# Low parts of the merge gates' weight slabs: an accumulating transfer in place of a subtraction

## The chip, the cores and the metric

The kernel runs on one core of a Trainium2 chip. Its time is the device time of one execution in microseconds (us), taken as the median over several runs. The names used below: PE is the matrix engine (PEld its weight loads), DVE the vector engine, ACT the scalar engine, POOL the GpSimd engine, SP the engine that issues most of the transfers. A line number such as L454 is a line of the kernel before.

## What is computed

One layer of a hybrid encoder: an input projection whose columns feed attention, a gated delta rule run in both directions, and two merge gates; the two branches are gated, summed and projected, and a second gated term is added. Cut to what bears on the change (512 positions, model width 1024, float32):

```python
h = rms_norm(x, norm_pre[i])
(aq, ak, av, az, dq, dk, dv, db, da, dz, gate_att, gate_dn) = split_cols(h @ w_in[i])
...
y_att = (o_att * jax.nn.silu(az)) @ w_br_att[i]
...
y_dn = (o_dn * jax.nn.silu(dz)) @ w_br_dn[i]
mix = (jax.nn.sigmoid(gate_att) * y_att + jax.nn.sigmoid(gate_dn) * y_dn) @ w_out[i]
x = x + rms_norm(mix, norm_post[i])
e = p[i] @ w_ple_proj[i]
x = x + rms_norm(jax.nn.sigmoid(x @ w_ple_gate[i]) * e, ple_norm[i])
```

`gate_att` and `gate_dn` are the two merge gates. Their weights are 2048 columns of `w_in`.

## The kernel before, in words

Every large product is made of three products in a shorter float format (float32r): a weight tile w is split into a high part `hi`, which is w rounded to that format, and a low part `lo` = w - `hi`; the activations are split in the same way, and PE adds lo x high, high x low and high x high into one accumulator.

**Slabs.** The weights come as 72 slabs of 128 columns (1024 x 128, as a tile of 128 x 1024 numbers, 512 KB), named by kind and number: dk, dq, dv, dz, az, gA (merge gate of the attention branch), gB (merge gate of the delta branch), ydn, yatt, with eight of each. Blocks of 512 columns (kv, q0, q1, out0, out1, pg0, pg1) come in four pieces of the same size each. `fetch` issues the loads into the tile `wraw` (two buffers) on SP's queue. `loader` follows: it takes one `whi` and one `wlo` buffer (two of each), calls `split`, which has ACT cast `wraw` to `whi` and then DVE or POOL subtract (`wlo` = `wraw` - `whi`), and gives `wraw` back. `gemm_t` runs a slab's 24 matmuls on PE, eight rounds of L454 (low part), L455 and L456 (high part), and gives `whi` and `wlo` back in the last round. `gemm_k` does so for kv and q0, q1 (L489 to L491), `gemm_n` for the last four blocks (L471 to L473), whose parts lie in buffers of their own (u).

**Order.** `ORDER` is a list written out by hand, by which one generator (`stream`) walks through the slabs and blocks, one after the other. Everything else (the delta rule's two chains, one for each group of four heads; attention; what follows each slab) is made of other generators. A planner in Python (`Flow`) runs them all against a clock of its own at build time: each operation is booked on its engine with an estimated duration, at the first gap that fits; a generator waits for events, for buffers (`get`) or for a time; among those that are ready the one with the lowest priority number goes first, and the stream has 10, the chains 1. The order of those bookings becomes the order of the instructions on each engine, which is then fixed; on the chip an instruction waits for its data by semaphores. A booking on both DVE and POOL (`W`) makes the planner keep both free, though only one of them works.

**Where a low part is made.** `split` with `sbuf=True` works out when the subtraction would end on DVE (1024 x 0.00113 us, with POOL kept free) and on POOL (1024 x 0.00232 us), and takes POOL if that ends sooner than the other way plus `COOL` (1.5 us), or plus `HOT` (0 us) while a chain's triangular solve is under way (`chains[0]`); in the first 20 us of the planner's clock always POOL (`slow`).

**The chains.** Each chain (one after the other) makes decay matrices (`phase_a`: transfers of CI, an addition on DVE, a select and a product on POOL, then matmuls L828 and L833), solves triangular systems with 30 dependent steps on DVE, and then runs `phase_b` (L985 to L1037). `phase_y` norms the chain's result and transposes it (L1095). The tails of q0 and q1 rotate and transpose (L1250), the convolutions' tails transpose (L686). After q1 the eight attention heads run (L1339), then the yatt slabs, out0, out1, pg0 and pg1. A merge gate's result goes through a tanh to the DRAM tensors gate_gA and gate_gB and is read back much later, in `ydn_tail` and `yatt_tail`.

**Norm vectors.** The item `vec` of `ORDER`, which stands after yatt5 and yatt6, starts two `vec_load` generators that load the weights of the last two norms into `blk` buffers (three in all, used by the heads as well). Each yatt job waits for `att_start` and for all eight heads before its matmuls.

Of the kernel before, what the change touches and what calls it, by code (L numbers as in the profile page):

```python
# [9 lines left out]
F32 = mybir.dt.float32  # L10
F32R = mybir.dt.float32r
AF = mybir.ActivationFunctionType
ALU = mybir.AluOpType
# [21 lines left out]
class Flow:  # L35
# [39 lines left out]
    def op(self, eng, dur, dep, fn, *a, **k):  # L75

        engs = eng if isinstance(eng, tuple) else (eng,)
        t, at = self.slot(engs, dur, dep)
        for e, i in zip(engs, at):
            self.eng[e].insert(i, (t, t + dur))  # L80
        if fn is not None:
            self.n += 1
            heapq.heappush(self.later, (t, self.n, fn, a, k))
        return t + dur

    def free(self, tag, t=None):
        self.slots[tag].append(self.now if t is None else t)
# [61 lines left out]
X_DVE = ()  # L149
WARM = 9  # L150
W1 = 0
COOL, HOT = 1.5, 0


@with_exitstack
def layer(ctx, tc, x, p, wt, wba, wn, wpp, npre, rows, qkn, hd16, npost, pnorm, dnorm, cs, out):
    nc = tc.nc
    pe, act, dve, pool, sync = nc.tensor, nc.scalar, nc.vector, nc.gpsimd, nc.sync

    caps = {"wraw": 2, "whi": 2, "wlo": 2, "f2": 5, "c2": 4, "blk": 3, "gi": 2, "go": 2, "mm": 5, "aux": 3}  # L160
    F = Flow({**caps, **{f"u{i}": 1 for i in range(17)}})
    op, free, spawn = F.op, F.free, F.spawn

    def A(dur, dep, fn, *a, **k):
        return op("ACT", dur, dep, fn, *a, **k)
# [8 lines left out]
    def G(dur, dep, fn, *a, **k):  # L174
        return op("POOL", dur, dep, fn, *a, **k)

    def Q(kb, dep, o, i):

        t = op("DGE", 0.46, dep, sync.dma_start, o, i)
        return op("DMA", kb * 0.364, t + 0.5, None) + 1.0  # L180

    sb = ctx.enter_context(tc.tile_pool(name="sb", bufs=1))
    ps = ctx.enter_context(tc.tile_pool(name="ps", bufs=1, space=bass.MemoryType.PSUM))
# [3 lines left out]
    def tile(tag, shape, dt=F32):  # L187
        cnt[0] += 1
        return sb.tile(list(shape), dt, tag=tag, bufs=caps.get(tag, 1), name=f"{tag}_{cnt[0]}")

    def const(shape, name, dt=F32):
        return sb.tile(shape, dt, tag=name, bufs=1, name=name)

    def unit(i, shape, dt=F32):
        return tile(f"u{i}", shape, dt)
# [12 lines left out]

    chains = [0]

    def split(src, hi, lo, dep, n, sbuf=False, slow=False):

        t = A(0.08 + n * 0.00085, dep, act.copy, hi, src)
        eng = "DVE"
        if sbuf:
            eng = ("DVE", "POOL")
            tv = F.slot(eng, n * 0.00113, t)[0] + n * 0.00113
            tp = F.slot(("POOL",), n * 0.00232, t)[0] + n * 0.00232
            if slow or tp < tv + (HOT if chains[0] else COOL):
                eng = "POOL"  # L220
        fn = (pool if eng == "POOL" else dve).tensor_sub
        t2 = op(eng, n * (0.00232 if eng == "POOL" else 0.00113), t, fn, lo, src, hi.bitcast(F32))
        return t, t2

    def bc(a):
        return a.unsqueeze(2).to_broadcast([128, 4, 128])
# [5 lines left out]
    def row(src, n):  # L232
        return src.rearrange("(o n) -> o n", o=1).broadcast_to([128, n])
# [12 lines left out]
    two = const([64, 32], "two")  # L246
# [35 lines left out]
    load, ple, late = {}, {}, {}  # L282
# [8 lines left out]
    def first_loads():  # L291
# [4 lines left out]
        def p_half(i):  # L296
            ple["tp"].append(Q(2, 0.0, ple["p"][:, 2 * i:2 * i + 2], p[256 * i:256 * i + 256].rearrange("(t p) n -> p t n", p=128)))
# [3 lines left out]
        def ple_weights(half):  # L301
            raw = tile("wraw", [128, 2, 512])
            load["ple", half] = raw, Q(4, 0.0, raw, wpp.rearrange("(j p) n -> p j n", p=128)[:, :, half * 512:half * 512 + 512])
            fetched["ple", half].set(F.now)

        def x_tile(t):
            if t % 2 == 0:
                xu.append(unit(4 + t // 2, [128, 2, D]))
            xt = xu[t // 2][:, t % 2, :]
            load["x", t] = xt, Q(4, 0.0, xt, x[t * 128:(t + 1) * 128, :])  # L310
# [24 lines left out]
    def h_part():  # L335
# [29 lines left out]
        for t in range(NT):  # L365
            xt = load["x", t][0]
            for half in range(2):
                yield "at", sc[t, half] + 0.3
                yield "get", "aux"
                pt = bank("aux", [128, 4, 128])  # L370
                for j in range(4):
                    k = half * 4 + j
                    pe.transpose(pt[:, j, :], xt[:, k * 128:(k + 1) * 128], ident)
                yield "pe", 0.45
                cc = slice(t * 128, (t + 1) * 128)
                _, te = split(pt, hTh[half][:, :, cc], hTl[half][:, :, cc], F.now, 512)
                free("aux", te)
                if t == NT - 1:
                    h_ev[half].set(te + 0.2)
# [17 lines left out]
    def fetch(names):  # L397
        for name in names:
            if name[0] == "ple":
                continue  # L400
            yield "get", "wraw"
            if name[0] == "blk":
                raw = tile("wraw", [128, 2, 512])
                j = name[2]
                src = wn[BLOCK_IDX[name[1]]][:, 2 * j:2 * j + 2, :]
            else:
                raw = tile("wraw", [128, 8, 128])
                src = wt[SLAB_IDX[name]]
            load[name] = raw, Q(4, 0.0, raw, src)
            fetched[name].set(F.now)  # L410

    def loader(names):
        for name in names:
            yield "ev", fetched[name]
            raw, t = load[name]
            sh = [128, 8, 128] if name[0] not in ("blk", "ple") else [128, 2, 512]
            if name[:2] in places or name[0] == "ple":
                if name[0] == "ple":
                    us = (7 + name[1], 7 + name[1])
                    yield "get", f"u{us[0]}"  # L420
                    w = unit(us[0], [128, 2, 2, 512], F32R)
                    hi, lo = w[:, 0], w[:, 1]
                else:
                    us, j = places[name[:2]], name[2]
                    his, los = blocks.setdefault(name[1], ([], []))
                    if j % 2 == 0:
                        for u, lst in ((us[j // 2], his), (us[j // 2 + 2], los)):
                            yield "get", f"u{u}"
                            lst.append(unit(u, [128, 4, 512], F32R))
                    a = (j % 2) * 2  # L430
                    hi, lo = his[-1][:, a:a + 2, :], los[-1][:, a:a + 2, :]
            else:
                yield "get", "whi"
                yield "get", "wlo"
                hi = tile("whi", sh, F32R)
                lo = tile("wlo", sh, F32R)
            yield "at", t - 0.3
            _, tl = split(raw, hi, lo, t, 1024, True, F.now < 20.0)
            free("wraw", tl)
            slab[name][0].set(tl + 0.2)  # L440
            slab[name][1] = (hi, lo)

# [121 lines left out]
    def decay():  # L564
# [4 lines left out]
        wb, t = load["wb"]  # L569
        ws = tile("f2", [128, 8, 64], F32R)  # L570
        _, t = split(wb, ws[:, :, 0:32], ws[:, :, 32:64], t, 256, True)
        free("f2", t)
        yield "at", t + 0.2
# [712 lines left out]
    head_ev = {}  # L1286
    att_start = Event()
# [168 lines left out]
        return rs, G(0.8, dep, fn)  # L1456

    def vec_load(name, src, scale=1.0):
        yield "get", "blk"
        v = late[name] = tile("blk", [128, D])  # L1460
        t = Q(4, 0.0, v, row(src, D))
        if scale != 1.0:
            yield "at", t - 0.5
            t = G(1.5, t, pool.tensor_scalar, out=v, in0=v, scalar1=scale, scalar2=0.0, op0=ALU.mult, op1=ALU.add)
        return t
# [144 lines left out]
    def late_vectors():  # L1610
        late["npo_ev"] = spawn(vec_load("npo", npost), 4)
        late["pno_ev"] = spawn(vec_load("pno", pnorm, 0.5), 4)
# [32 lines left out]
    for n in names:  # L1645
        slab[n] = [Event(), None]
        fetched[n] = Event()
    spawn(fetch(names), 2)
    spawn(loader(names), 2)

    def stream():
# [57 lines left out]
```

## Time and profile before

| | us |
|---|---|
| median of 3 runs (lowest, highest) | 807.49 (805.36, 807.97) |
| the profiled execution's own time | 806.62 |
| its span, first to last instruction | 804.9 |
| PE busy | 764.8 |
| DVE busy | 485.5 |
| POOL busy | 354.0 |
| ACT busy | 316.4 |

The mean granted PE clock of the profiled execution is 0.984 of full speed. Transfers move 96.69 MB, and their packets take 37.8% of the 16 transfer engines' span. The span is what the profiler saw between the first and the last instruction; the execution's own time is 1.7 us longer. In rows of the time line the columns are the start in us, the duration in us, engine, line and operation, what is written and what is read, and in brackets the engine's idle time before it and what ended that. Many operations are recorded by one helper, so that their line is L101; the tile's name tells them apart.

### The profile page before, as it was taken

To read this page: it belongs to the slowest core of one execution; us is meant where nothing else is said; L and a number is where in the kernel's file an instruction comes from. 1 tells how busy PE (TensorE), PEld (TensorE's weight loads), DVE (VectorE), ACT (ScalarE), POOL (GpSimd) and SP (SyncE) were. 2 spreads that over 40 slices of the span, in tenths; PEclk is the share of its full clock that TensorE was granted. 3 is DMA by queue.
4 is the path that set the end of the run, shared out by engine and by line. 5 is a ranking of instruction groups with operands and counts; after the bars stand their busy time and mean duration, and the time that the engine had idled before them with its cause. 6 is when DMAs were issued, how large, how long until landed. Compare 5 with 4: busy or idle time off the path is not lost.

```text
span 804.9 us, 11746 instructions
## 1 busy us (share of the span) xinstructions
PE 764.8 (95%) x4522; PEld 634.8 (79%) x4522; DVE 485.5 (60%) x902; ACT 316.4 (39%) x522; POOL 354.0 (44%) x305
## 2 busy tenths in 40 slices
PE   8998999999999996999999989898999999799995
PEld 6787888887888975878787877686888888678884
DVE  4466777978667567596748554638656633723434
ACT  6454514336334143233452233334656533331421
POOL 6344492014125359502522257655566464560431
PEclk9999999999999998999999999999999999899998
DMA  7372226453212271645411232333253347643213
GB/s 258 114 216 92 78 86 164 126 174 95 67 31 75 79 198 64 170 143 165 133 41 52 80 110 80 105 104 105 79 178 110 118 145 245 207 132 122 92 40 130
DMA packets 52969, 96.69 MB, mean 120 GB/s; under 512 B 20849, under 2 KB 22449, under 8 KB 52914
## 3 DMA queue, kind: packets, MB, share of 16 engines
q1 hardware_dynamic: 52914, 95.95, 37.8%
q8 instruction: 35, 0.57, 0.3%
q14 instruction: 20, 0.16, 0.1%
HBM read 79.12 MB, written 16.81 MB: 119 GB/s over the span
## 4 chain that ended last, share of the span: by engine, by line
PE 75%; DVE 9%; DMA 5%; POOL 4%; issue 3%; ACT 3%; SPq 0%; POOLq 0%; DVEq 0%; ACTq 0%
PE mm L454 12%; PE mm L456 12%; PE mm L455 12%; PE mm L471 4%; PE mm L473 4%; PE mm L472 4%; DVE f L101 4%; PE mm L489 2%; PE mm L491 2%; PE mm L490 2%; DVE u L101 2%; POOL u L101 2%; PE mm L1339 2%; PE aux L1005 2%; PE aux L1037 2%
## 5 line engine op out<-in xcount | busy, mean ns | idle before, releaser
L101 POOL TENSOR_TENSOR wlo<-wraw,whi 128x1024 fp32r<-128x1024 f32 x70 | 168.1, 2403 | 294.7 <-ACT whi L101 291.1
L454 PE MATMUL mm<-u,wlo 128*128 128x512 f32 x576 | 233.5, 405 | 5.6 <-POOL wlo L101 5.6
L456 PE MATMUL mm<-u,whi 128*128 128x512 f32 x576 | 225.6, 392 | 0.0
L455 PE MATMUL mm<-u,whi 128*128 128x512 f32 x576 | 225.0, 391 | 0.0
L101 ACT CAST whi<-wraw 128x1024 fp32r<-128x1024 f32 x84 | 88.2, 1050 | 165.2 <-PE mm L456 106.4
L454 PEld LDWEIGHTS mm<-u,wlo 128*128 128x128 f32 x576 | 108.7, 189 | 26.6 <-POOL wlo L101 6.9
L456 PEld LDWEIGHTS mm<-u,whi 128*128 128x128 f32 x576 | 108.4, 188 | 23.7
L455 PEld LDWEIGHTS mm<-u,whi 128*128 128x128 f32 x576 | 108.8, 189 | 19.6
L101 DVE SCALAR_TENSOR_TENSOR f<-mm,cw,f 128x510 f32<-128x510 f32 (+1 forms) x96 | 71.9, 748 | 23.5 <-ACT f L101 21.0
L471 PE MATMUL mm<-u,u 128*128 128x512 f32 x128 | 51.6, 403 | 4.8 <-DVE u L101 4.8
L101 POOL TENSOR_TENSOR u<-wraw,u 128x1024 fp32r<-128x1024 f32 x18 | 44.4, 2474 | 16.3 <-ACT u L101 16.1
L473 PE MATMUL mm<-u,u 128*128 128x512 f32 x128 | 50.6, 396 | 0.0
L472 PE MATMUL mm<-u,u 128*128 128x512 f32 x128 | 50.5, 395 | 0.0
L101 DVE TENSOR_TENSOR u<-aux,u 128x512 f32<-128x512 f32 (+1 forms) x48 | 32.0, 688 | 22.7 <-ACT u L101 12.5
L101 ACT ACTIVATE f<-mm 128x512 f32<-128x512 f32 (+1 forms) x44 | 24.8, 579 | 48.6 <-PE mm L473 39.9
L489 PE MATMUL mm<-whi,u 128*128 128x512 f32 x96 | 39.2, 408 | 0.0
L490 PE MATMUL mm<-wlo,u 128*128 128x512 f32 x96 | 38.0, 396 | 1.2 <-POOL wlo L101 1.2
L491 PE MATMUL mm<-whi,u 128*128 128x512 f32 x96 | 38.1, 396 | 0.0
L471 PEld LDWEIGHTS mm<-u,u 128*128 128x128 f32 x128 | 24.4, 191 | 10.6 <-DVE u L101 5.8
L101 ACT COPY c<-aux 128x512 f32<-128x512 f32 x18 | 10.7, 592 | 49.9 <-DVE f L101 23.2
L101 DVE TENSOR_TENSOR blk<-mm,blk 128x512 fp32r<-128x512 f32 x32 | 21.2, 687 | 12.9 <-ACT blk L101 12.9
L473 PEld LDWEIGHTS mm<-u,u 128*128 128x128 f32 x128 | 24.4, 191 | 5.4
(253 smaller groups left out, 1296.9 us busy)
## 6 DMA issues: line engine op xcount, KB each, us to landing
wraw<-in_wt_dram SPq DMA_DIRECT2D x72, 512.0 KB, 3.4
wraw<-in_wn_dram SPq DMA_DIRECT2D x28, 512.0 KB, 3.9
u<-CI SPq DMA_DIRECT2D x16, 256.0 KB, 6.1
u<-in_x_dram SPq DMA_DIRECT2D x4, 512.0 KB, 7.7
eD<-c SPq DMA_DIRECT2D x8, 256.0 KB, 2.2
gate_az<-go SPq DMA_DIRECT2D x8, 256.0 KB, 3.4
gate_dz<-go SPq DMA_DIRECT2D x8, 256.0 KB, 2.1
gate_gB<-go SPq DMA_DIRECT2D x8, 256.0 KB, 2.0
```

The costliest lines, as they stand in the source:

```text
L101: fn(*a, **k)
L454: pe.matmul(o, lo[:, k, :], mh(k), start=(k == 0), stop=False)
L455: pe.matmul(o, hi[:, k, :], ml(k), start=False, stop=False)
L456: pe.matmul(o, hi[:, k, :], mh(k), start=False, stop=(k == 7))
L471: pe.matmul(o, b, hi, start=(k == 0), stop=False)
L472: pe.matmul(o, a, lo, start=False, stop=False)
L473: pe.matmul(o, a, hi, start=False, stop=(k == 7))
L489: pe.matmul(o[t], b, hi, start=(k == 0), stop=False)
L490: pe.matmul(o[t], a, lo, start=False, stop=False)
L491: pe.matmul(o[t], a, hi, start=False, stop=(k == 7))
L1005: pe.matmul(pw[:, h, :], Vm[g][d][:, 4 * c + h, :], r[:, h, :], start=True, stop=True)
L1037: pe.matmul(oa[:, h, :], AT[g][d][:, 4 * c + h, :], w[:, h, :], start=True, stop=True)
```

## The change

For slabs of the kinds gA and gB, once the planner's clock is past 30 us, a third way of making the low part stands beside the two subtractions. ACT casts `wraw` to `whi` as before, and `wraw` is given back at once. ACT then writes -`whi` into `wlo`, and POOL issues a transfer that reads the slab from DRAM a second time and adds it into `wlo`. `BIAS` is added to the planned end of each way (DVE, POOL, transfer; the first triple outside a triangular solve, the second during one), and the earliest wins; the transfer has -9 us in both. The planner books for it 0.95 us of ACT, 1.1 us of POOL, and 2.9 us of the transfer engines with 0.65 us ahead and 1.5 us behind.

The other slabs choose between DVE and POOL as before; the rule that forces POOL in the first 20 us is gone, and the planned durations are rounded (0.9504 to 0.95, 1.157 to 1.16, 2.376 to 2.38). `vec_load` waits for `att_start` and for the eight heads. `ORDER` is the same.

```diff
-COOL, HOT = 1.5, 0
+BIAS = ((1.5, 0, -9), (0, 0, -9))
+BYDMA = ("gA", "gB")
...
+    def P(kb, dep, o, i):
+
+        t = op("POOL", 1.1, dep, pool.dma_start, o, i, accum_op=ALU.add)
+        return op("DMA", 2 * kb * 0.364, t + 0.5, None) + 1.5
+
...
-    def split(src, hi, lo, dep, n, sbuf=False, slow=False):
+    def split(src, hi, lo, dep, n, sbuf=False):
 
         t = A(0.08 + n * 0.00085, dep, act.copy, hi, src)
-        eng = "DVE"
-        if sbuf:
-            eng = ("DVE", "POOL")
-            tv = F.slot(eng, n * 0.00113, t)[0] + n * 0.00113
-            tp = F.slot(("POOL",), n * 0.00232, t)[0] + n * 0.00232
-            if slow or tp < tv + (HOT if chains[0] else COOL):
-                eng = "POOL"
-        fn = (pool if eng == "POOL" else dve).tensor_sub
-        t2 = op(eng, n * (0.00232 if eng == "POOL" else 0.00113), t, fn, lo, src, hi.bitcast(F32))
-        return t, t2
+        return t, (W if sbuf else V)(n * 0.00113, t, dve.tensor_sub, lo, src, hi.bitcast(F32))
...
-            load[name] = raw, Q(4, 0.0, raw, src)
+            load[name] = raw, Q(4, 0.0, raw, src), src
...
             yield "at", t - 0.3
-            _, tl = split(raw, hi, lo, t, 1024, True, F.now < 20.0)
-            free("wraw", tl)
+            th = A(0.95, t, act.copy, hi, raw)
+
+            two = ("DVE", "POOL")
+            ends = [F.slot(two, 1.16, th)[0] + 1.16 + BIAS[min(chains[0], 1)][0], F.slot(("POOL",), 2.38, th)[0] + 2.38 + BIAS[min(chains[0], 1)][1]]
+            if name[0] in BYDMA and F.now > 30.0:
+                ta = F.slot(("ACT",), 0.95, th)[0] + 0.95
+                tp = F.slot(("POOL",), 1.1, ta)[0] + 1.6
+                ends.append(F.slot(("DMA",), 2.9, tp)[0] + 4.4 + BIAS[min(chains[0], 1)][2])
+            way = ends.index(min(ends))
+            if way == 2:
+                free("wraw", th)
+                tl = A(0.95, th, act.mul, lo, hi.bitcast(F32), -1.0)
+                tl = P(4, tl, lo, load[name][2])
+            else:
+                tl = op((two, "POOL")[way], (1.16, 2.38)[way], th, (dve, pool)[way].tensor_sub, lo, raw, hi.bitcast(F32))
+                free("wraw", tl)
             slab[name][0].set(tl + 0.2)
...
     def vec_load(name, src, scale=1.0):
+        yield "ev", att_start
+        for h in range(8):
+            yield "ev", head_ev[h]
         yield "get", "blk"
```

`split` is also called for tiles of 256 and 512 numbers that are no weights (activations in SBUF with `sbuf=True`). There the choice between DVE and POOL falls away: the subtraction is booked on both and runs on DVE.

More of the change, by code (lines that the diff above doesn't have):

```diff
@@ L414, in loader @@
             yield "ev", fetched[name]
-            raw, t = load[name]
+            raw, t = load[name][:2]
             sh = [128, 8, 128] if name[0] not in ("blk", "ple") else [128, 2, 512]
```

## The prediction

> **What bounds the kernel now.** I read the page first, then PE's waits, then the tile wraw (through which every weight slab passes), and last the time line around single merge-gate slabs.
>
> ```profile
> PE 764.8 (95%) x4522; PEld 634.8 (79%) x4522; DVE 485.5 (60%) x902; ACT 316.4 (39%) x522; POOL 354.0 (44%) x305
> ```
> ```profile
> PE aux L833 <- DVE u L101: 6.5, 2, 5.9
> PE mm L454 <- POOL wlo L101: 5.6, 4, 2.0
> PE mm L471 <- DVE u L101: 4.8, 1, 4.8
> PE mm L1095 <- DVE u L101: 3.5, 4, 1.1
> PE mm L1250 <- DVE f L101: 2.5, 2, 1.4
> ...
> PE mm L490 <- POOL wlo L101: 1.2, 1, 1.2
> PE mm L686 <- DVE f L101: 0.9, 1, 0.9
> ```
>
> PE is busy 764.8 of 804.9 us. The 40 us it lacks are all there is to win, and 4.8 of them lie ahead of out0 (L471), behind the last gate slab. In the list of waits (us in total, times, longest) PE waits for low parts made on POOL for only 5.6 + 1.2 us. POOL and DVE, which the change relieves, are half idle. So the question is whether a gate slab's low part, made the new way, is there when PE wants it.
>
> ```profile
> L101 ACT CAST whi<-wraw x84: 1027/1052/1088, 18.4 to 688.1; 128x1024 fp32r<-128x1024 f32 x84
> ...
> L101 POOL TENSOR_TENSOR wlo<-wraw,whi x70: 2342/2396/2825, 19.6 to 689.2; 128x1024 fp32r<-128x1024 f32 x70
> ...
> L101 DVE TENSOR_TENSOR wlo<-wraw,whi x14: 1217/1223/1226, 133.7 to 371.2; 128x1024 fp32r<-128x1024 f32 x14
> ...
> DMA to landing us min/median/max: 3.0/3.7/8.8
> ```
>
> Today a low part costs 1.05 us on ACT and then 2.40 on POOL or 1.22 on DVE. How long it may take is set by the two whi/wlo buffers: the cast starts when PE has left the slab before last, and PE wants the result when it leaves the last one. Slabs are told apart by counting PE's groups of eight L454 along ORDER. Rows of gB6 (cast, subtraction, first matmul), then cast and first matmul of gA7, gA4, gB3 and gB0, and between them the cast of gB7:
>
> ```profile
> 149.68 0.39 PE L454 MATMUL mm<-u,wlo 128*128 128x512 f32 x1
> 149.88 1.05 ACT L101 CAST whi<-wraw 128x1024 fp32r<-128x1024 f32 x1 [1.69 <-PE mm L456]
> 150.97 1.23 DVE L101 TENSOR_TENSOR wlo<-wraw,whi 128x1024 fp32r<-128x1024 f32 x1 [0.60 <-ACT whi L101]
> 155.12 0.39 PE L454 MATMUL mm<-u,wlo 128*128 128x512 f32 x1
> 160.76 1.06 ACT L101 CAST whi<-wraw 128x1024 fp32r<-128x1024 f32 x1 [3.89 <-PE mm L456]
> 166.00 0.39 PE L454 MATMUL mm<-u,wlo 128*128 128x512 f32 x1
> 335.85 1.05 ACT L101 CAST whi<-wraw 128x1024 fp32r<-128x1024 f32 x1 [3.90 <-PE mm L456]
> 341.04 0.39 PE L454 MATMUL mm<-u,wlo 128*128 128x512 f32 x1
> 342.59 1.05 ACT L101 CAST whi<-wraw 128x1024 fp32r<-128x1024 f32 x1 [5.20 <-DMA wraw<-in_wt_dram]
> 498.72 1.05 ACT L101 CAST whi<-wraw 128x1024 fp32r<-128x1024 f32 x1 [3.21 <-PE mm L491]
> 503.92 0.39 PE L454 MATMUL mm<-u,wlo 128*128 128x512 f32 x1
> 536.35 1.05 ACT L101 CAST whi<-wraw 128x1024 fp32r<-128x1024 f32 x1 [4.39 <-PE mm L491]
> 541.55 0.39 PE L454 MATMUL mm<-u,wlo 128*128 128x512 f32 x1
> ```
>
> In each pair 5.2 us lie between the cast and PE's first matmul (155.12 - 149.88 = 5.24, 541.55 - 536.35 = 5.20). A slab occupies PE 5.44 us (149.68 to 155.12, the slab ahead of gB6). Where PE does nothing but slabs, that is the whole window. Eight gate slabs stand so: these five, and gB7, gA1 and gA0, which follow gA4. Ahead of the other eight, PE has other work between the slabs and the window is longer, except at gA6, of which below.
>
> **The change part by part.** Removed: five subtractions on DVE (gB6, gA7, gB7, gA1, gA0), 5 x 1.22 = 6.1 us, and eleven on POOL, 11 x 2.40 = 26.4 us. PE waited for none of them except gA6's, so I take no gain; the bounds follow with the rivals. Added for each of 16 slabs: a second ACT pass of the cast's shape (1.05; 16.8 us in all, covered by ACT's 61% idle; without that cover up to these 16.8 return), one issue on POOL's queue, and a transfer of 512 KB that reads HBM a second time and adds into wlo.
>
> Moved: `split` loses its choice for its other callers too, so the low parts of the normed delta result and of the heads' outputs go from POOL to DVE:
>
> ```profile
> L101 DVE TENSOR_TENSOR blk<-mm,blk 128x512 fp32r<-128x512 f32 x32 | 21.2, 687 | 12.9 <-ACT blk L101 12.9
> L101 POOL TENSOR_TENSOR u<-f,u 128x512 fp32r<-128x512 f32 x16 | 21.0, 1316 | 13.7 <-ACT u L101 13.7
> ```
>
> POOL loses 21.0 us, DVE takes 16 x 0.69 = 11 (0.69 by the first row, the same subtraction on DVE). PE waits for none of the 16; DVE has 40% idle. I take 0; without that cover at most 11 us, and the 16 x 0.63 us by which each is sooner at best.
>
> The accumulating transfer is in no row. From below it is a plain load of the same size, 3.0 to 3.7 us from issue to landing; from above the slowest such load, 8.8. Two more rows (KB each, us to landing) tell what twice the bytes costs:
>
> ```profile
> gate_gB<-go SPq DMA_DIRECT2D x8, 256.0 KB, 2.0
> ...
> dW<-blk SPq DMA_DIRECT2D x2, 512.0 KB, 4.0
> ```
>
> 256 KB more cost 2.0 us. The accumulation moves 512 KB in and as much out of wlo; in full sequence that is 3.7 + 4.0 = 7.7 us, in full overlap 3.7. I take 5.5, near the middle. The way from cast to low part is then 1.05 + 0.08 + 1.05 + 0.08 + 5.5 = 7.8 us (0.08: the hand-over 149.88 + 1.05 to 150.97, rounded up), between 5.3 and 11.1. Against 5.2 PE waits 2.6 us (0.1 to 5.9).
>
> gB6 and gA7: 2.6 each, with a slab of the old way between them. In the run gA4, gB7, gA1, gA0 every late slab also shifts the next: gA4 2.6 late, start 343.6, end 349.1; gB7, cast at 342.59, is there at 350.4, 1.3 late; gA1 1.2 and gA0 1.3 by the same steps; 6.4 together. gB3 and gB0: 2.6 each. Sum 16.8 us.
>
> Not all of it reaches the end, because PE idles a little later anyway, for work that does not depend on the slab.
>
> ```profile
> 297.45 0.50 PE L454 MATMUL mm<-u,wlo 128*128 128x512 f32 x1 [1.34 <-POOL wlo L101]
> ...
> 310.02 2.08 PE L833 MATMUL aux<-u,u 128*128 128x128 f32 x8 [5.92 <-DVE u L101]
> ...
> 549.51 0.50 PE L454 MATMUL mm<-u,wlo 128*128 128x512 f32 x1 [1.42 <-POOL wlo L101]
> ```
>
> Behind gB3 come L490's 1.2 and an L1250 wait of 1.4: covered. Behind gB0 come 1.42 and the other 1.1: 2.5 covered. Behind the run of four come 0.9 (L686) and four L1095 waits, 3.5: 4.4 covered. Behind gB6 and gA7 I count only the 1.34; the 5.92 us hole at 304 to 310 belongs to the chain's L833, and the planner, which also counts the slab as late, puts it behind those matmuls. Covered 1.3 + 4.4 + 2.6 + 2.5 = 10.8; left 6.0 us.
>
> Idle PE also costs clock (columns: PE busy, PEld, DVE, ACT, POOL, clock, DMA share, GB/s):
>
> ```profile
> 60.00:80.00 20.00, 17.96 (x76) 14.46 (x75) 13.73 (x19) 9.57 (x15) 9.16 (x6) 0.91 0.28 93
> 300.00:320.00 20.00, 12.70 (x68) 10.90 (x66) 15.44 (x25) 6.46 (x11) 17.24 (x17) 0.83 0.25 84
> 480.00:500.00 20.00, 16.61 (x71) 13.26 (x72) 8.58 (x10) 5.86 (x8) 15.16 (x13) 0.91 0.32 106
> 540.00:560.00 20.00, 17.33 (x82) 13.36 (x81) 16.71 (x28) 6.96 (x12) 12.00 (x16) 1.00 0.40 132
> ```
>
> From 60 to 80 us PE has one wait, 20 - 17.96 = 2.04 us, and a clock of 0.91: 0.09 x 20 = 1.8 us more. The 1.42 at 548 cost no clock. Five of the new stalls are single ones of 2.6. I price three of them at 1.8, as they lie just above that edge, and take off the 1.8 at 480 to 500, whose gap fills: +3.6 (0 to +9.0). [...]
>
> gA6 is alone. POOL is full ahead of its subtraction:
>
> ```profile
> 306.88 8.02 POOL L101 TENSOR_TENSOR u<-u,Nj 128x512 f32<-128x512 f32 x8
> 314.86 2.35 POOL L101 TENSOR_TENSOR wlo<-wraw,whi 128x1024 fp32r<-128x1024 f32 x1
> ```
>
> If the issue takes the subtraction's place behind the eight products, the low part lands at 314.9 + 5.5 = 320.4 instead of 317.2: 3.2 us worse. If it comes ahead of them, part of PE's hole fills. I take 0.
>
> New waits: the issue waits on POOL for the second ACT pass, and POOL's next work (the chain's selects and products, other slabs' subtractions) stands behind it, up to 1.1 us each time; POOL's 56% idle covers it, and POOL loses 26.4 us here, against 16 issues of unknown length. SP: a gate slab's wraw is free after the cast, 2.5 us sooner, so the next load goes out sooner and runs beside the accumulation. Both then share the 16 engines; that is in the 5.5. The dropped `slow` rule and the rounded durations can move a slab of the first 20 us: 0, within 1 us. vec_load's waits change nothing, since "vec" stands behind yatt5 and yatt6 in ORDER, which wait for the same eight heads.
>
> Sum: 6.0 + 3.6 = +9.6 us on the profiled 806.62 (span 804.9 and 1.7 around it): 816.2. The median of the runs is 807.49, 0.9 above, so 816 to 817.
>
> **The rivals.** Hidden anyway (17%): the transfer lands like a plain load, 3.0 to 3.7 us, the stalls are 0.1 to 0.8 us and the later idle swallows them; 805.5 to 808.5. For it: the least landing; against: a read and a write of wlo come on top. Fewer than 16 transfers (4%) ends there too: the planner could pick a subtraction, but its -9 makes that rare.
>
> Nothing covered (12%): the order is planned anew, the later gaps stay, every stall counts: 16.8 + 5 x 1.8 + 3.2 = +29, 836. [...]
>
> ```profile
> 195.00:555.00 360.00, 337.30 (x2385) 284.16 (x2384) 227.25 (x446) 120.96 (x185) 153.87 (x125) 0.99 0.33 100
> ```
>
> Faster (28%): the chain is what the late stalls fall against. Two DVE subtractions (gB6, gA7) leave the first triangular solve, so the chain is up to 2.4 us earlier at 310, and the stalls fall wholly into the 360 - 337.3 = 22.7 us that PE idles between 195 and 555. Then no stall counts, the clock drops at 300 to 320 (0.17 x 20 = 3.4) and 480 to 500 (1.8) go: 806.6 - 2.4 - 5.2 = 799. It decides if the new order closes the 5.92 us hole at L833. For it: the hole is larger than both stalls of the first solve. Against: PE's order is fixed, so a late slab must stand ahead of L833 to fill it.
>
> **How the numbers follow.** The forecast has 39% (811 to 824 for itself, the landing at 4.5 to 6.5 us). Three runs span 0.3%, and that is what counts as no change: 805.1 to 809.9. Faster: 28%. Same: the 21% of the hidden cases less a part that ends above, 16%. Slower: 56%. The range 799 to 832 leaves out most of the case with nothing covered and the faster half of the fast one.
>
> **What would show it.** Right: PE's first L454 of gB6, gA7, gA4, gB3 and gB0 waits 2 to 3 us for a DMA into wlo; DVE 5 us more (11 - 6.1), POOL 47 us less save for what the issues take, ACT 17 more; 8.4 MB more read; PE's waits at L490, L1250 and L1095 shrink. Wrong: landings under 4 us with L454 never waiting for wlo; or L833's 5.9 us gone, with a clock of 1.00 around 300.

## The result, and the profile after

The changed kernel takes 832.12 us (median of 4 runs, 830.72 to 836.2) against 806.91 for the kernel before (4 runs): 1.0322 times as long, 95% interval 1.0282 to 1.0363, or 25.2 us more. One run of all those below (959.71 us, of the kernel in which only the choice in `split` is taken out) ran at a clock of 0.751 and is left out of that kernel's figures. The profiled execution is the longest of the four, 836.2 us with a span of 834.5; its terms are compared with those of the 804.9 us span before, and stand about 4 us above the median. Lines of the changed kernel are numbered 11 higher: L465 is L454 of before, L844 is L833.

The page's first line, its part on queues and its groups, and PE's list of waits (us in total, times, longest):

```profile
PE 778.0 (93%) x4522; PEld 643.3 (77%) x4522; DVE 483.1 (58%) x911; ACT 332.5 (40%) x539; POOL 325.7 (39%) x295
...
q0 software_dynamic: 2304, 8.39, 6.0%
...
L101 POOL DMA_DIRECT2D wlo<-in_wt_dram x16 | 14.5, 908 | 108.7 <-ACT wlo L101 79.0
...
wlo<-in_wt_dram POOLq DMA_DIRECT2D x16, 512.0 KB, 6.0
```
```profile
PE mm L465 <- DMA wlo<-in_wt_dram: 16.7, 7, 4.1
PE mm L465 <- POOL wlo L101: 8.3, 3, 5.7
PE mm L465 <- DVE f L101: 5.1, 1, 5.1
...
PE aux L839 <- DVE u L101: 2.8, 1, 2.8
PE mm L1261 <- DVE f L101: 2.0, 2, 1.0
...
PE aux L844 <- DVE u L101: 1.4, 1, 1.4
...
PE mm L1106 <- DVE u L101: 0.3, 1, 0.3
```

All 16 slabs go by transfer (x16, 8.39 MB). PE executes the same 4522 matmuls. The span grew by 29.6 us, in two parts: PE idle 834.5 - 778.0 = 56.5 us, 16.4 more than the 40.1 of before; and PE busy 778.0, 13.2 more. The instructions are the same, so this is put down to the granted clock (0.984 before, 0.966 here): the lost share of the span went from 0.016 x 804.9 = 12.9 to 0.034 x 834.5 = 28.4 us, 15.5 more, and part of that falls into PE's waits, where it costs nothing. The new entry is L465 waiting for the transfer, 16.7 us in seven waits. The 5.1 us put down to DVE is an eighth, as the rows of gA4 show. The time line of gB6 (with the first matmul behind its wait), of gA4, and the first matmuls of the other late slabs, in the columns explained before the prediction:

```profile
149.56 1.05 ACT L101 CAST whi<-wraw 128x1024 fp32r<-128x1024 f32 x1 [1.69 <-PE mm L467]
150.65 1.06 ACT L101 ACTIVATE wlo<-whi 128x1024 fp32r<-128x1024 f32 x1
152.02 0.95 POOL L101 DMA_DIRECT2D wlo<-in_wt_dram  x1 [21.07 <-ACT wlo L101]
158.08 0.80 PE L465 MATMUL mm<-u,wlo 128*128 128x512 f32 x1 [3.12 <-DMA wlo<-in_wt_dram]
176.17 0.80 PE L465 MATMUL mm<-u,wlo 128*128 128x512 f32 x1 [4.11 <-DMA wlo<-in_wt_dram]
...
356.54 0.88 POOL L101 DMA_DIRECT2D wlo<-in_wt_dram  x1 [4.59 <-ACT go L101]
364.36 0.76 PE L465 MATMUL mm<-u,wlo 128*128 128x512 f32 x1 [5.14 <-DVE f L101]
381.60 0.50 PE L465 MATMUL mm<-u,wlo 128*128 128x512 f32 x1 [3.47 <-DMA wlo<-in_wt_dram]
495.73 0.80 PE L465 MATMUL mm<-u,wlo 128*128 128x512 f32 x1 [3.50 <-DMA wlo<-in_wt_dram]
536.37 0.77 PE L465 MATMUL mm<-u,wlo 128*128 128x512 f32 x1 [1.58 <-DMA wlo<-in_wt_dram]
```
```profile
DMA to landing us min/median/max: 1.9/5.5/7.7
```

From gB6's cast to its first matmul pass 158.08 - 149.56 = 8.5 us; before it was 5.2. gA4's issue starts at 356.54 and its low part is read at 364.36, 7.8 us later, which fits the longest landing of the tile wlo, 7.7; the profile names DVE because the wait is for several semaphores. In order: gB6 3.12, gA7 4.11, gA4 5.14, gA1 3.47, gB5 3.50, gB3 1.58; the rest of the 21.8 us (16.7 + 5.1) lies at gB0 and gA3. The matmul behind five of these waits takes 0.76 to 0.80 us instead of the 0.39 of L454 before: PE comes back at half clock (157.3 to 164.0 us, the start of it still in gB6's wait, has a granted clock of 0.50). By stage (PE busy, PEld, DVE, ACT, POOL, clock, DMA share, GB/s):

```profile
140.00:180.00 40.00, 32.77 (x126) 26.11 (x125) 29.42 (x69) 12.02 (x16) 1.81 (x2) 0.84 0.55 151
195.00:555.00 360.00, 329.64 (x2440) 277.27 (x2439) 218.00 (x440) 129.18 (x193) 124.83 (x107) 0.96 0.39 109
340.00:400.00 60.00, 51.39 (x215) 41.60 (x214) 33.46 (x81) 17.39 (x22) 12.42 (x9) 0.91 0.63 160
480.00:500.00 20.00, 16.50 (x77) 13.46 (x76) 14.68 (x32) 7.53 (x13) 11.25 (x11) 0.91 0.52 138
```

The waits of gB6 and gA7, 7.2 us of idle PE (40 - 32.77), come with 0.16 x 40 = 6.4 us of lost clock in the same stretch; where no slab is late, 150 to 175 us runs at 1.00 without a gap, as a row of the experiments shows. Those of gA4 and gA1 (8.6 us) come with 0.09 x 60 = 5.4 us, gB5's 3.5 with 0.09 x 20 = 1.8, which the kernel before lost in the same stretch too (0.91 at 480 to 500 in the prediction's rows).

### The profile page after: what moved, and what is told of

Same layout as the page of the kernel before. It is cut to its first block, busy times and chain, and to the rows that moved or that the text cites. A ratio compares the mean times of both kernels' runs of the same rounds, so it can differ in the third digit from the quotient of the medians.

```text
span 834.5 us, 11805 instructions
## 1 busy us (share of the span) xinstructions
PE 778.0 (93%) x4522; PEld 643.3 (77%) x4522; DVE 483.1 (58%) x911; ACT 332.5 (40%) x539; POOL 325.7 (39%) x295
## 3 DMA queue, kind: packets, MB, share of 16 engines
q0 software_dynamic: 2304, 8.39, 6.0%
## 4 chain that ended last, share of the span: by engine, by line
PE 71%; issue 7%; DMA 7%; DVE 6%; ACT 5%; POOL 4%; SPq 0%; POOLq 0%; DVEq 0%; ACTq 0%
PE mm L465 11%; PE mm L466 11%; PE mm L467 11%; DMA wlo<-in_wt_dram 4%; PE mm L482 4%; PE mm L484 4%; PE mm L483 4%; DVE f L101 3%; PE mm L500 2%; PE mm L502 2%; PE mm L501 2%; POOL wlo L101 2%; DVE u L101 2%; PE aux L1016 2%; ACT whi L101 2%
## 5 line engine op out<-in xcount | busy, mean ns | idle before, releaser
L465 PE MATMUL mm<-u,wlo 128*128 128x512 f32 x576 | 239.2, 415 | 30.1 <-DMA wlo<-in_wt_dram 16.7
L101 POOL TENSOR_TENSOR wlo<-wraw,whi 128x1024 fp32r<-128x1024 f32 x62 | 148.8, 2400 | 238.7 <-ACT whi L101 218.6
L467 PE MATMUL mm<-u,whi 128*128 128x512 f32 x576 | 230.3, 400 | 0.0
L466 PE MATMUL mm<-u,whi 128*128 128x512 f32 x576 | 230.2, 400 | 0.0
L465 PEld LDWEIGHTS mm<-u,wlo 128*128 128x128 f32 x576 | 112.2, 195 | 55.1 <-DMA wlo<-in_wt_dram 15.9
L467 PEld LDWEIGHTS mm<-u,whi 128*128 128x128 f32 x576 | 111.6, 194 | 25.1
L466 PEld LDWEIGHTS mm<-u,whi 128*128 128x128 f32 x576 | 112.3, 195 | 21.1
L101 POOL DMA_DIRECT2D wlo<-in_wt_dram x16 | 14.5, 908 | 108.7 <-ACT wlo L101 79.0
L101 POOL TENSOR_TENSOR u<-wraw,u 128x1024 fp32r<-128x1024 f32 x17 | 42.0, 2476 | 16.6 <-ACT u L101 16.5
L482 PEld LDWEIGHTS mm<-u,u 128*128 128x128 f32 x128 | 24.5, 192 | 10.8 <-DVE u L101 6.0
```

The lines of the kernel that those rows point to most:

```text
L101: fn(*a, **k)
L465: pe.matmul(o, lo[:, k, :], mh(k), start=(k == 0), stop=False)
L466: pe.matmul(o, hi[:, k, :], ml(k), start=False, stop=False)
L467: pe.matmul(o, hi[:, k, :], mh(k), start=False, stop=(k == 7))
L482: pe.matmul(o, b, hi, start=(k == 0), stop=False)
```

## The experiments

Theory A: PE's waits for the late low parts, with the half clock that follows them, make the loss. Its main rival: the other edits and the newly planned order make it, and the waits only stand where other waits would. Further questions are how much of A is clock, how much is the accumulation, and which slabs count. Ratios are to the kernel before, measured beside each run; the diffs are against the changed kernel unless another base is named.

**Without the transfers.** Everything but the transfer is kept.

```diff
-BYDMA = ("gA", "gB")
+BYDMA = ()
```

> The changed kernel with no slab allowed the transfer (BYDMA empty); its other edits stay: the split's other callers on DVE, the dropped rule for the first 20 us, rounded durations, vec_load's waits. Theory A (the 25 us are PE's waits for the accumulating transfers, some 22 us in eight waits, and the half clock behind them, some 10 to 13 us, less some 5 to 10 of earlier idle that goes): 804 to 810 us, clock back at 0.98. Rival B (the loss is the new order and the moved subtractions): 820 to 832, clock near 0.97.

Measured: 813.81 us (9 runs), ratio 1.0076 (1.0045 to 1.0107). Some 18 us of the loss go with the transfers. About 7 us stay, more than theory A allowed, so the other edits had to be taken apart.

**The choice in `split` put back as well.**

```diff
-BYDMA = ("gA", "gB")
+BYDMA = ()
+COOL, HOT = 1.5, 0
...
-    def split(src, hi, lo, dep, n, sbuf=False):
+    def split(src, hi, lo, dep, n, sbuf=False, slow=False):
...
+            if slow or tp < tv + (HOT if chains[0] else COOL):
+                eng = "POOL"
```

> No slab by transfer, and split's old choice between DVE and POOL restored for its other callers (the 16 subtractions of 512 numbers can go to POOL again); the dropped rule for the first 20 us, the rounded durations and vec_load's waits stay as in the changed kernel. Of the 7 to 8 us that the kernel with no transfer is over the kernel before: if the moved subtractions make them, 804 to 808. If the small edits to the planner's numbers make them, 811 to 816.

Measured: 805.09 us (12 runs) against 806.76, ratio 0.9989 (0.9972 to 1.0006). The rounded durations, the dropped `slow` rule and the waits in `vec_load` together cost nothing that can be measured.

**Only that choice taken out** (base: the kernel before). The 16 subtractions of activations go from POOL to DVE, and nothing else changes.

```diff
-            if slow or tp < tv + (HOT if chains[0] else COOL):
-                eng = "POOL"
...
+        return t, (W if sbuf else V)(n * 0.00113, t, dve.tensor_sub, lo, src, hi.bitcast(F32))
```

> The mirror of it: the kernel before with nothing but split's choice taken from its other callers (they are booked on DVE and POOL and run on DVE); the weight slabs choose as before. If the moved subtractions make the 7 to 8 us: 811 to 816, with a granted clock of 0.98 or less. If not: 804 to 808.

Measured: 811.68 us (median of five runs) against 806.76, ratio 1.0071 (1.005 to 1.0091). The moved subtractions cost about 5 us by themselves. Its page and its waits:

```profile
PE 765.8 (95%) x4522; PEld 634.6 (78%) x4522; DVE 500.8 (62%) x919; ACT 316.5 (39%) x521; POOL 335.7 (41%) x289
```
```profile
PE aux L828 <- DVE u L101: 7.9, 3, 6.0
...
PE mm L681 <- DVE f L101: 3.8, 2, 3.3
```

DVE carries 15 us more than the 485.5 of before, and two places where PE already waited for DVE wait longer: L681 (L686 of before) 3.8 instead of 0.9, L828 (L833 of before) 7.9 instead of 6.5; together 4.3 us. PE's busy time hardly moves.

**The transfers alone.** The choice in `split` is back, as in the second experiment, and BYDMA stays as in the changed kernel.

```diff
 BYDMA = ("gA", "gB")
+COOL, HOT = 1.5, 0
```

> All 16 gate slabs by transfer as in the changed kernel, but split's old choice restored for its other callers. The two parts measured so far are +7 us (edits without transfer) and +18 (the rest). If they add up: 821 to 827 us. If the moved subtractions cost nothing once the transfers have made PE late: 829 to 833.

Measured: 832.87 us against 806.24, ratio 1.0327 (1.0297 to 1.0357): the whole loss, and not the part beyond the 7 us. PE's waits:

```profile
PE mm L475 <- DMA wlo<-in_wt_dram: 22.4, 10, 4.9
PE mm L475 <- POOL wlo L101: 7.1, 2, 5.6
```

The two edits do not add up. With the transfers in place the moved subtractions cost nothing more, and with the subtractions back PE waits as long for the transfers as in the changed kernel, 22.4 us against 21.8.

**The eight slabs that the prediction called tight, and the eight others.** Two kernels, both with the choice in `split` back. Names are compared as kind and number (`name[0] + str(name[1]) in BYDMA`).

```diff
-BYDMA = ("gA", "gB")
+BYDMA = ("gB6", "gA7", "gA4", "gB7", "gA1", "gA0", "gB3", "gB0")
```

> The other half: gB6, gA7, gA4, gB7, gA1, gA0, gB3 and gB0 by transfer, the rest by subtraction. Theory A: nearly all of the loss, 816 to 823 us, with four to six waits of 2.5 to 5 us for a transfer into wlo and a granted clock of 0.975 or less. If the loss is spread evenly: 811 to 815.

```diff
-BYDMA = ("gA", "gB")
+BYDMA = ("gB1", "gB4", "gA5", "gA6", "gA2", "gA3", "gB5", "gB2")
```

> As the kernel with the transfer alone, for gB1, gB4, gA5, gA6, gA2, gA3, gB5 and gB2 only: the slabs ahead of which PE had other work before. Theory A (only the pure slab stretches wait): 804 to 809 us, at most one stall over 2 us. If every transfer costs 1 us or more wherever it stands (the order, the engines shared): 813 to 817.

Measured: tight 833.39 us, ratio 1.0353 (1.0288 to 1.0418); loose 806.96 us (10 runs), ratio 1.0012 (0.9996 to 1.0028). First the waits of the kernel with the tight eight and its stage around gB6 and gA7, then the same two of the one with the loose eight:

```profile
PE mm L475 <- DMA wlo<-in_wt_dram: 17.4, 6, 4.6
PE mm L1116 <- DVE u L101: 9.4, 8, 3.2
```
```profile
150.00:175.00 25.00, 17.05 (x66) 13.19 (x66) 18.69 (x47) 6.29 (x9) 1.95 (x2) 0.92 0.64 161
```
```profile
PE aux L854 <- DVE u L101: 7.6, 3, 5.8
...
PE mm L475 <- DMA wlo<-in_wt_dram: 1.3, 1, 1.3
```
```profile
150.00:175.00 25.00, 25.00 (x112) 20.67 (x112) 22.21 (x52) 6.19 (x8) 0.00 (x0) 1.00 0.47 161
```

Eight transfers where PE does nothing but slabs cost the whole 27 us; eight where it has other work between the slabs cost nothing, though each reads, adds and queues just the same. The loss is therefore neither the bytes, nor the second ACT pass, nor POOL's issue, but the place. The tight eight came out above the 816 to 823 expected: besides the 17.4 us for the transfers, L1116 (L1095 of before) waits 9.4 us instead of 3.5. Whether the late slabs or the newly planned order make that was not separated, so the 27 us are not all waits for a transfer.

**The low part used last.** All 16 transfers stay; `gemm_t` runs a gate slab's 16 matmuls with the high part first and the eight with the low part behind them, so PE needs the transfer some 3.6 us later (16 x 0.227 us by the plan).

```diff
+LAST = BYDMA
...
+        if name[0] in LAST:
+            yield "ev", slab[name][2]
...
+                pe.matmul(o, hi[:, k, :], ml(k), start=(k == 0), stop=False)
+                pe.matmul(o, hi[:, k, :], mh(k), start=False, stop=False)
...
+            yield "ev", slab[name][0]
+            for k in range(8):
+                pe.matmul(o, lo[:, k, :], mh(k), start=False, stop=(k == 7))
```

> The changed kernel; for gA and gB alone the 16 matmuls with the high part run first and the eight with the low part last, so that the low part is wanted 3.6 us later (16 x 0.227). Theory A: the window grows from 5.2 to 8.8 us and holds the 8.3 that cast, negation and a 6.0 us transfer take: waits for wlo fall from 22 to under 5 us, clock 0.98, 804 to 811 us. Rival C (the transfers cost by what they share: POOL's queue, the transfer engines, the order): 820 or more.

Measured: 813.68 us (10 runs), ratio 1.0088 (1.0066 to 1.011), above the 804 to 811 expected, which had left out the moved subtractions. That is the time of the kernel without transfers and with the same `split` (1.0076). PE waits for a transfer twice:

```profile
PE mm L475 <- DMA wlo<-in_wt_dram: 4.8, 2, 3.7
```

With the waits nearly gone, the transfers cost nothing beyond the moved subtractions. (What this order of matmuls would bring in the gate slabs without transfers was not measured; before, only gA6 of them waited, 0.82 us.) This and the pair before it decide for A.

**A plain copy in place of the accumulation.** Order and engines stay as in the changed kernel; the gate slabs' low part is then the weight itself.

```diff
-        t = op("POOL", 1.1, dep, pool.dma_start, o, i, accum_op=ALU.add)
+        t = op("POOL", 1.1, dep, pool.dma_start, o, i)
```

> The changed kernel, every engine's order the same, with the 16 transfers on POOL's queue as plain copies instead of accumulations (the low part of the gate slabs is then the weight itself, so the gates come out otherwise). It prices the accumulation. If reading wlo back is what makes them land after 6.0 us (median): landing 4.0 to 4.5, each of eight stalls 1.5 to 2 shorter, 813 to 820 us. If the way over POOL is what takes the time: landing 5.5 to 6.0, 828 to 833.

Measured: 823.06 us, ratio 1.0195 (1.0141 to 1.0249), 9 us less than the changed kernel. From its page and its waits:

```profile
wlo<-in_wt_dram POOLq DMA_DIRECT2D x16, 512.0 KB, 4.9
```
```profile
PE mm L465 <- DMA wlo<-in_wt_dram: 12.3, 5, 3.0
```

The addition costs 6.0 - 4.9 = 1.1 us of landing, between the two cases expected; 0.3 of it lies in POOL's issue, which takes 0.60 us here on average instead of 0.91. Over all the slabs that wait this adds up: the waits for the transfer fall from 21.8 to 12.3, and PE's busy time by 1.5. But even without the addition the way is too long for these slabs.

**The negated copy first.** ACT writes -`wraw` into `wlo` ahead of the cast, so the transfer is issued one ACT pass sooner.

```diff
-                tl = A(0.95, th, act.mul, lo, hi.bitcast(F32), -1.0)
-                tl = P(4, tl, lo, load[name][2])
+                tn = A(0.95, t, act.mul, lo, raw, -1.0)
+                th = A(0.95, tn, act.copy, hi, raw)
...
+                tl = max(th, P(4, tn, lo, load[name][2]))
```

The row of this pass (ACTIVATE wlo<-wraw, 128x1024 fp32r<-128x1024 f32) writes the short format as the cast does, so `wlo` holds the rounded -`wraw`; that this equals -`whi` is taken, not shown.

> The changed kernel; for the gate slabs ACT writes the negated cast into wlo first, straight from wraw, and casts to whi after that, so that the transfer is issued 1.1 us sooner and still adds the same numbers. Theory A (each of some eight stalls is the 8.3 us way less the 5.2 us window): each stall 1.1 us shorter, waits for wlo 22 down to 13, half the clock loss gone, 816 to 825. If the transfers queue behind something else (POOL, the transfer engines): 829 to 833.

Measured: 828.13 us, ratio 1.0266 (1.0244 to 1.0288), only 4 us less, outside the 816 to 825 expected. The waits and the landing:

```profile
PE mm L461 <- DMA wlo<-in_wt_dram: 12.4, 6, 3.1
...
PE mm L1102 <- DVE u L101: 5.3, 5, 2.8
```
```profile
wlo<-in_wt_dram POOLq DMA_DIRECT2D x16, 512.0 KB, 6.7
```

PE waits 9.4 us less for the transfers. Landing takes 0.7 us longer, and L1102 (L1095 of before), which waited 0.5 us in the changed kernel and 3.5 before, waits 5.3. So such waits take back a part of what the earlier transfers gain.

**PE kept busy while it waits.** Ahead of six late slabs PE runs 24 transposes of a constant, whose result is overwritten.

```diff
+FILL = ("gB6", "gA7", "gA4", "gA1", "gB5", "gB3")
...
+        if name[0] in BYDMA and name[0] + str(name[1]) in FILL:
+            yield "get", "mm"
+            o = bank("mm")
+            for _ in range(24):
+                pe.transpose(o[:, 0:128], ident, ident)
+            yield "pe", 2.6
+            yield "ev", slab[name][0]
```

> The changed kernel with 24 small transposes (about 2.6 us, result unused) put on PE ahead of six gate slabs that wait (gB6, gA7, gA4, gA1, gB5, gB3). PE loses the same time, but isn't idle in it. Theory A, part clock (half-clock stretches behind the stalls cost about 10 us): 819 to 825, granted clock 0.98. Rival (the idle alone costs, the clock nothing): 830 to 836.

Measured: 832.45 us, ratio 1.0298 (1.0244 to 1.0352), against 819 to 825 expected of A. The page, the fillers' group and the waits:

```profile
PE 786.3 (95%) x4666; PEld 655.3 (79%) x4666; DVE 483.6 (58%) x911; ACT 333.0 (40%) x539; POOL 324.4 (39%) x295
```
```profile
L463 PE MATMUL mm<-ident 128*128 128x128 f32 x144 | 16.7, 273 | 0.0
```
```profile
PE mm L474 <- DMA wlo<-in_wt_dram: 9.0, 8, 2.0
```

The clock came back (0.982 in this profile), and without its fillers PE is busy 786.3 - 16.7 = 769.6 us, 8.4 less than in the changed kernel. But the fillers took 16.7 us of PE to replace 12.8 us of waits (21.8 to 9.0). The run shows that the half clock hangs on PE's idling in the waits (mean clock 0.982 against 0.966 in the changed kernel), not that the time could be had back this way.

**The kernel before, low part last in all 128-column slabs** (base: the kernel before; no transfers).

```diff
+LAST = ("dk", "dq", "dv", "dz", "az", "gA", "gB", "ydn", "yatt")
```

> The kernel before with the low part's eight matmuls last in every slab of 128 columns, no transfer. If late low parts are what leaves PE idle between the slabs (waits for POOL's wlo 5.6 us, and the clock behind the one of 2 us): 799 to 804. If the gaps are the chain's: 805 to 808, the same as before.

Measured: 796.78 us (6 runs) against 806.76, ratio 0.9887 (0.9858 to 0.9916). Its page:

```profile
PE 764.9 (96%) x4522; PEld 635.3 (79%) x4522; DVE 487.1 (61%) x899; ACT 319.2 (40%) x524; POOL 356.2 (45%) x306
```

L454's 5.6 us of waits for low parts are gone, and in a span of 799.9 us PE is idle for 35. It beats both kernels, and by more than the 799 to 804 expected; a part of this may come from the newly planned order.

**Transfers and low part last in all slabs**, with the choice in `split` back.

> All 16 gate slabs by transfer, split's old choice restored, and the low part's matmuls last in every slab of 128 columns. The kernel before with low parts last ran in 796.8. Theory A: the transfers are hidden (way 8.3 us, window 8.8) and POOL and DVE have 32 us less to do, so 793 to 800. If a hidden transfer still costs by what it shares: 802 to 808.

Measured: 819.21 us, ratio 1.0152 (1.0118 to 1.0185), far from the 793 to 800 expected. The waits:

```profile
PE mm L729 <- DVE f L101: 9.1, 2, 6.1
...
PE mm L485 <- DMA wlo<-in_wt_dram: 2.7, 2, 2.5
```

The transfers are hidden (2.7 us). Against the kernel before with low parts last, whose profiled span is 799.9 us, PE is idle 43.2 us instead of 35.0 and busy 774.6 instead of 764.9 (clock 0.970 against 0.982). The wait of 6.1 us lies at 104 us, where PE did not wait in the kernel before, and one operation of a convolution's tail on DVE makes it. First its row and POOL's rows here, then its row in the kernel before with low parts last:

```profile
99.94 9.93 DVE L101 SCALAR_TENSOR_TENSOR f<-f,f 128x512 f32<-128x512 f32 x1 [0.16 <-ACT f L101]
98.75 8.28 POOL L101 TENSOR_TENSOR u<-u,Nj 128x512 f32<-128x512 f32 x8
106.73 2.58 POOL L101 TENSOR_TENSOR wlo<-wraw,whi 128x1024 fp32r<-128x1024 f32 x1
```
```profile
99.39 1.93 DVE L101 SCALAR_TENSOR_TENSOR f<-f,f 128x512 f32<-128x512 f32 x1 [0.17 <-ACT f L101]
```

The same operation takes 0.69 us in the kernel before. Here it starts while POOL works without a break until 109.31, and ends 0.56 us behind that; there it starts beside a subtraction of POOL that ends at 100.77, and ends 0.55 us behind it. The kernel before has the like: DVE's SCALAR_TENSOR_TENSOR u<-u,f at 63.56 us takes 1.66 us (the fifteen others 0.70 on average) beside a subtraction of POOL that ends at 64.67, and ends 0.55 us behind it. So it seems to stand still for as long as POOL goes on; no run tests this by itself. In the newly planned order gB1's issue (97.93) has taken the place of that subtraction, and the eight products follow at once. The rest of the 22 us over 796.78 stays unexplained: the run shows that a transfer can cost through the order that is planned around it, but not how much.

## Why the prediction was wrong

It forecast 816 us, slower, and the kernel is slower; but 832.12 lies just above the range, and the loss is 25.2 us instead of 9.6. The sign and the mechanism held. The step that failed is the sizing of the sum's terms: the clock behind the stalls (3.6 for 13.2), the gross waits (16.8 for 21.8) and the surroundings of gA6 (nothing for 2.6), while less than forecast was covered. The sum in the profiled runs, span against span; the changed kernel's is the longest of its four runs:

| term, us | predicted | measured |
|---|---|---|
| waits for the late low parts | 16.8 | 21.8 |
| gA6 and the hole at the first chain | 0 | 2.6 |
| covered by later idle time | -10.8 | -8.0 |
| PE idle in all | 6.0 | 16.4 |
| clock | 3.6 | 13.2 |
| sum | 9.6 | 29.6 |

- **Which slabs: right in the main.** The eight tight ones alone make the whole loss (1.0353), the eight others none (1.0012). In the changed kernel itself six of the tight eight waited; gB7 and gA0 did not, and gB5, counted as loose, waited 3.5 us just where the four L1095 waits, 3.5 us before, shrank to 0.5 (0.3 in the row shown). That gB5's wait took their place is a reading of the two lists; with the loose eight alone no such wait appeared.
- **The way from cast to low part: a little short.** 7.8 us predicted, 8.5 measured at gB6: the issue started 0.3 us behind the ACT pass, not 0.08 (152.02 - 151.71), and landing took 6.0, not 5.5. The gross stalls were 21.8 us instead of 16.8. The two bounds of the landing, 3.7 and 7.7, held the median.
- **Covered by later idle: right in kind, too high by 2.8.** L490's 1.2 and most of the L1095 waits are gone, as forecast. The L686 and L1250 waits stayed at 1.1 and 2.0, where 0.9 and 2.5 were to go. The measured 8.0 is what remains: 21.8 + 2.6 - 16.4.
- **gA6 at nothing: failed.** POOL's issue did stand behind the eight products, as the unfavourable case had it, and the waits around them grew: before, L833's 6.5 and an L454 wait of 0.8, together 7.3; after, L465's longest wait for POOL, L839 and L844, 5.7 + 2.8 + 1.4 = 9.9. The long one lies at the slab ahead of gA6 (dv6), whose subtraction POOL makes late: its cast ends at 301.60, but in POOL's new order seven selects of the chain, which wait for DVE, stand ahead of it. gA6 itself did not wait. So it is the order, not the issue's place, that cost here. One row of the kernel before (the 0.8), then four of the changed one:

```profile
317.27 0.50 PE L454 MATMUL mm<-u,wlo 128*128 128x512 f32 x1 [0.82 <-POOL wlo L101]
```

```profile
314.41 2.35 POOL L101 TENSOR_TENSOR wlo<-wraw,whi 128x1024 fp32r<-128x1024 f32 x1
316.82 0.79 PE L465 MATMUL mm<-u,wlo 128*128 128x512 f32 x1 [5.69 <-POOL wlo L101]
...
317.99 8.03 POOL L101 TENSOR_TENSOR u<-u,Nj 128x512 f32<-128x512 f32 x8
325.96 0.90 POOL L101 DMA_DIRECT2D wlo<-in_wt_dram  x1
```

The 2.6 us lie under the bound of 3.2, which was meant for gA6's own low part; that is luck.

- **Clock +3.6: failed, in the profiled run the largest miss of a single term.** There it was 13.2 us of longer matmuls, above the bound of 9.0. For the median, 25.2 less the 16.4 of idle leaves an estimated 9, if the idle time was the same. The price of 1.8 us for three single stalls came from one stall of 2.04 us, which drew a half-clock stretch of 3.41 us; behind the stalls of gB6, gA7 and gA4 it lasted 6.83 us each. And the 1.8 us taken off for 480 to 500 did not go, as gB5's stall stands there now. The new stalls of 3.1 to 5.1 us cost 6.4 us for two (140 to 180) and 5.4 for two (340 to 400). gB3's wait of 1.58 us, shorter than that one of 2.04, drew a half-clock stretch of 3.41 us too. And with one order of instructions the clock varies from run to run: 836.2 us at 0.966, the other three 830.7 to 832.2 at 0.972.
- **The moved subtractions at nothing: wrong alone, right here.** They cost about 5 us in the kernel before, within the bound of 11, and nothing beside the transfers. The rows that said "PE waits for none of the 16" said nothing on what stands behind them on DVE.
- **The other small edits at nothing: right** (0.9989).
- **The engines' load: near, but for DVE.** ACT has 16.1 us more and 8.39 MB more are read, as forecast. DVE was to have 5 us more and has 2.4 less: its subtractions into `wlo` fell from 14 to 6, not by five, and POOL's from 70 to 62, not by eleven, as the other slabs chose anew. POOL, without the new issues, has 42.8 us less (354.0 - 325.7 + 14.5), where 47 was forecast.
- **The rivals.** "Nothing covered", 836 us at a chance of 12%, came closest, but not by its mechanism: 8.0 us were covered, and its number is near because stalls and clock were larger than it had them. "Hidden anyway" fell with the landing of 6.0. "Faster" needed the hole at the chain closed; the waits around it grew.

## What to carry to other kernels

Before a step on a double-buffered path is made longer, measure the window from buffer free to first use at every place it occurs: eight transfers cost nothing and eight others 27 us, at the same work. Where a product is a sum of several, let PE take the operand that is ready last at the end; that alone hid these transfers (PE waited 4.8 us for them instead of 21.8) and brought 1.1% in the kernel before. And a stall of some microseconds on a busy PE is priced with the half clock behind it, which here came to more than half of its length again (1.8 us for a wait of 3.5, 6.4 for two of 7.2 together).

## What the runs showed of the hardware

- 512 KB took, median from issue to landing, 3.4 us from SP's queue (`wraw`, in the changed kernel), 4.9 from POOL's as a plain copy and 6.0 with the addition (6.7 in the kernel with the negated copy first). POOL is busy 0.91 us with each accumulating issue and 0.60 with each plain one.
- Waits of 3 to 5 us on PE came with lost clock of half to nine tenths of their own length (1.8 for 3.5, 5.4 for 8.6, 6.4 for 7.2); some of it falls into the wait itself.
- The clock recorded in the traces of the kernel before and of the changed one is full or half (1.00 or 0.50), nothing between. The half-clock stretches last 3.41 or 6.83 us. Ahead of the one that ends each trace the kernel before has four, 20.5 us in all, and the changed kernel ten, 51.2 us: 15.4 us more lost, much as by the mean clock (15.5). A wait of 1.58 us was followed by 3.41, waits of 3.12, 4.11 and 5.14 by 6.83, those of 3.47 and 3.50 by 3.41 again, and the 1.42 of before by none: the length of the wait alone does not fix the loss.
- With the order of instructions fixed, a kernel's time goes with its mean clock, loosely: of 18 runs of the kernel before in one batch the shortest took 804.52 us at 0.986 and the longest 812.64 at 0.978, but others 805.95 at 0.982 and 807.45 at 0.987.
